# Transposes ahead of value products and scores in attention's lists, and keys' transposes ahead of intra-chunk products in the mixer

## The chip, the core and the metric

The kernel runs on one core of a Trainium2 chip. Such a core has a matrix engine (TensorE, PE in the profile; its weight loads are listed apart as PEld), a vector engine (VectorE, DVE), a scalar engine for activation functions (ScalarE, ACT), a general engine (GpSimd, POOL), and a sync engine (SP) that issues most DMAs. Each engine works through its own list of instructions in order and waits for semaphores of the others. Operands lie in SBUF; PE writes its results to PSUM, which has eight banks of 128 partitions x 512 floats, and from there ACT or DVE copy them out.

The metric is the device time of one execution, in microseconds (us); lower is better.

## The reference

Two layers of a decoder trunk on a sequence of 1024 positions and 1024 features. Layer 0 mixes tokens by dilated sliding-window attention, layer 1 by a gated linear recurrence (HGRN2) in chunks of 64; each mixer is followed by a squared-ReLU MLP, and each of the four sub-layers by a LayerNorm of the scaled input plus its output. What the change touches is inside the two mixers:

```python
def dilated_attention_mixer(x, w_in, w_out):
    proj = (x @ w_in).reshape(B, S, N_GROUPS, 3, ATTN_HEADS, ATTN_HEAD_DIM)
...
    for g, (window, dilation) in enumerate(DILATED_PATTERNS):
        q = rotary(proj[:, :, g, 0], pos)
        k = rotary(proj[:, :, g, 1], pos)
        o, lse = dilated_window_attention(q, k, proj[:, :, g, 2], window, dilation)
...
    wts = jax.nn.softmax(jnp.stack(lses, axis=0), axis=0)
    o = jnp.einsum('gbsh,gbshe->bshe', wts, jnp.stack(outs, axis=0).astype(F32))
    return o.reshape(B, S, ATTN_HEADS * ATTN_HEAD_DIM).astype(x.dtype) @ w_out

# in dilated_window_attention, on banded blocks of 128 queries
    s = jnp.einsum('znqhe,znkhe->znhqk', qb, kk).astype(F32) * (E ** -0.5)
    p = jnp.exp(s - m)
    o = jnp.einsum('znhqk,znkhe->znqhe', (p / l).astype(v.dtype), vv)

# in hgrn2_mixer, per head and chunk
    a = jnp.where(causal, jnp.einsum('bhcid,bhcjd->bhcij', q_dec, k_dec), 0.0)
    o_intra = jnp.einsum('bhcij,bhcje->bhcie', a, v)
    kv = jnp.einsum('bhcjd,bhcje->bhcde', key * jnp.exp(b_last - b), v)
```

## The kernel before

Dense products run in three passes of split floats (high x high, high x low, low x high), each a matmul of 128x128 weights with 512 columns. The rest of PE's work is small matmuls and transposes in full floats (a transpose is a matmul with the identity on the whole array).

**Attention.** The input projection is a list of products (`seq`, function `product`, L816), in each of which PE issues twelve matmuls (L826 to L828) into one of three `mm` banks. Heads are taken in pairs (8 of them), and a pair in one dilation group is a *unit*: 24 units, always in the order group 2, group 1, group 0. Two units make one round of 21 products (three outputs of seven products each). Work on units whose projection is done is put between the products: a table `fill` says for each product number which functions run behind it, a *slot*. A unit begins with step 0 four (first of a round) or fourteen (second) products into the next round and does one step every two or three products after it; the offsets are `OFFS` (L66), plus `UNIT0`. So step 5 of one unit and step 0 of the next fall into the same slot, the older unit first. The last round has no products behind it; its two units use a list of their own (the branch `tail` in `pieces`) in the output projection.

The six steps of a unit are the lists that `pieces` (L539) returns. They are made of:

- `vtrans`: eight transposes of the values, four to a `pt` bank, which ACT copies to `vn` (L551, L552).
- `qk` (L561) or, for group 2, `qk16` (L592): scores as small matmuls on a 64x64 part of the array (L573, L601) into two `s` banks; DVE adds the mask and takes the extreme (L586, L604) into a `p` tile, one of three; ACT takes the exponential with its row sum (L589, L608).
- `ptr` (L636), `ptr16` (L612): transposes of `p` into a `pt` bank (L642, L617), one of two, which ACT copies to a `pts` tile, one of four.
- `pv` (L647), `pv16` (L621): value products on 128x64 and 64x64 parts (L671, L673, L629) into the one `o` bank (`pv16` takes a `pt` bank too); ACT copies it out. `first` are blocks 0 to 3, `second` blocks 4 to 7.
- `shift`: three DMAs on the sync queue that make a copy of the values shifted by 64 rows.

PE and DVE are held to program order throughout the attention's main loop (`in_order`, L902); ACT's PSUM copies are held in the order of their making (`behind`, L986), and where else ACT stands is chosen by the framework's scheduler, which orders by program order and readiness.

**Mixer.** Per head there are six projections of 24 matmuls (L192 to L194), and between them the pieces of the head before (`head_pieces`, L1751): transposes of values and keys (`trans`, L1760, two `pt` banks each, copied by ACT), intra-chunk products (`amat`, L1768, one `s` bank, then DVE), chunk states (`kv`, L1784), outputs (`omat`, L1806, L1811) and their transposes (`otr`, L1833). Here PE's order is not written out; the scheduler chooses it. The pieces of the last head run in the output projection.

Of the kernel before, what the change touches and what calls it, by code (L numbers as in the profile page):

```python
# [69 lines left out]
def trunk_kernel(  # L70
# [32 lines left out]
    def U(name, dt=F32):  # L103
        return up.tile([P, 1024], dt, name=name, tag="u")

    def bank(tag, name):
        return ps.tile([P, 512], F32, name=name, tag=tag, bufs={"mm": 3, "s": 2, "pt": 2, "o": 1}[tag])
# [45 lines left out]
    one = cp.tile([P, 1], F32, name="one")  # L153
# [203 lines left out]
    def attention(pre, hc):  # L357
# [181 lines left out]
        def pieces(pr, g, qT, kT, vT, og, sS, tail):  # L539
# [145 lines left out]
            def qks(*tiles):  # L685
                return [lambda: qk(*tiles)]

            def run(f, bs):
                return [lambda b=b: f(b) for b in bs]

            one = [(b,) for b in range(8)]
# [8 lines left out]
                ]  # L700
            first, second = [lambda: pv(0, 1, 2, 3)], [lambda: pv(4, 5, 6, 7)]
            if g == 2:
                return [run(qk16, (0,)) + [vtrans], run(qk16, (1,)) + run(ptr16, (0,)), run(ptr16, (1,)),
                        [pv16], [], []]
            if g == 1:
                return [qks((0, 2), (4, 6)) + [vtrans], [shift] + qks((1,), (3,)) + run(ptr, ((0, 2), (4, 6))),
                        qks((5,), (7,)) + run(ptr, ((1,), (3,))), first + run(ptr, ((5,), (7,))), [], second]
            return [qks(*one[0:2]) + [vtrans], [shift] + qks(*one[2:4]) + run(ptr, one[0:2]),
                    qks(*one[4:6]) + run(ptr, one[2:4]), first + qks(*one[6:8]) + run(ptr, one[4:6]),
                    run(ptr, one[6:8]), second]  # L710

        def combine_tr(pr, g, slot, ml, tail):
# [153 lines left out]
        def unit_work(gi, a, base):  # L866
# [14 lines left out]
            def begin():  # L881
                ogs[pr][g] = U("og")
                p = pieces(pr, g, res.pop((a, 0)), res.pop((a, 1)), ep.pop((gi, 2, a)), ogs[pr][g], sS, last)
                for f in p[0]:
                    f()
                work.extend(p[1:])
# [855 lines left out]
    def hgrn(xs, late, consts, pre, gw):  # L1742
# [8 lines left out]
        def head_pieces(hd, kd, kd2, qd, vT, dec, oNt):  # L1751
            st = {}

            def trans(src, name):
                d = U(name)
                for j in range(2):
                    pt = bank("pt", "hpt")
                    for i in range(4):
                        b = j * 4 + i
                        nc.tensor.transpose(pt[:, i * P:(i + 1) * P], src[:, b * P:(b + 1) * P], ident)  # L1760
                    act(d[:, j * 512:(j + 1) * 512], pt, AF.Copy)
                st[name] = d
# [12 lines left out]
            def kv(j):  # L1775
                if j == 0:
                    st["S"] = [U("stA"), U("stB")]
                kb = [bank("s" if j else "pt", "kvps") for _ in range(2)]
                cs = [c for c in range(j * 8, j * 8 + 8) if c < NCH - 1]
                for c in cs:  # L1780
                    r = slice((c % 2) * CH, (c % 2) * CH + CH)
                    t = c // 2
                    for m in range(2):
                        nc.tensor.matmul(kb[c % 2][m * CH:m * CH + CH, (t % 4) * P:(t % 4 + 1) * P],  # L1784
                                         st["k2n"][r, t * P + m * CH:t * P + m * CH + CH],
                                         st["vn"][r, t * P:(t + 1) * P], start=True, stop=True, skip_group_check=True)
                for c in cs:
                    dst = state(c + 1)
                    kvc = kb[c % 2][:, (c // 2 % 4) * P:(c // 2 % 4 + 1) * P]
                    if c == 0:  # L1790
                        nc.vector.tensor_copy(dst, kvc)
                    else:
                        nc.vector.scalar_tensor_tensor(dst, state(c), dec[:, c:c + 1], kvc,
                                                       op0=ALU.mult, op1=ALU.add)
# [34 lines left out]
            def otr(j):  # L1829
# [8 lines left out]
            amats = [amat]  # L1838
            keys = lambda: trans(kd2, "k2n")
            return [  # L1840
                [lambda: trans(vT, "vn")] + (amats + [keys] if hd else [keys] + amats),
                [lambda: kv(0)],
                [lambda: omat(0), lambda: kv(1)],
                [lambda: omat(1)],
# [45 lines left out]
        for hd in range(8):  # L1890
# [29 lines left out]
            oNt = U("oN")  # L1920
            oN.append(ond[1, hd] if hd < SPILL[1] else oNt)
            new = head_pieces(hd, cur["kd"], cur["kd2"], cur["qd"], e[2], cur["dec"], oNt)
            if hd == 0:
                new = [[]] + new
# [110 lines left out]
```

## Time and profile before

| what | value |
|---|---|
| median of three runs | 2728.11 us (2725.67 to 2728.45) |
| the profiled execution, its own time | 2729.02 us |
| its span, first to last instruction | 2727.2 us |
| mean granted TensorE clock | 0.998 |
| attention's main loop, 80 to 905 us | PE busy 821.57 of 825.00 us, DVE 649.55, ACT 460.66 |
| mixer, 1680 to 2060 us | PE busy 379.04 of 380.00 us, DVE 225.62, ACT 199.88 |

The two rows by stage are from the view of busy time by stretches. A busy PE in that view isn't a PE at its best: matmuls overlap, so an engine that starts a matmul later than it could still counts as busy while the one before drains. What a border between two kinds of work costs has to be read from the distance between starts, in the timeline.

### The profile page before, as it was taken

What the parts mean: (1) busy time and instruction counts of PE and PEld (TensorE: products, weight loads), DVE (VectorE), ACT (ScalarE), POOL (GpSimd) and SP (SyncE); (2) the same over time, 40 slices, a digit from 0 to 9 for tenths busy, and PEclk for the clock granted to TensorE, in tenths of its full rate; (3) what the DMA queues carried; (4) which work ended last, traced back from release to release, by engine and by line L of the source; (5) the groups of instructions that cost most, each with busy time, mean ns of one, the idle gap of its engine ahead of it and who ended that gap; (6) DMA issues with size and microseconds to landing.
All of it is one profiled execution on the core that took longest, in us unless ns stands there. A gap on an engine that the chain in (4) does not pass through costs nothing.

```text
span 2727.2 us, 44137 instructions
## 1 busy us (share of the span) xinstructions
PE 2698.6 (99%) x16256; PEld 2199.0 (81%) x16256; DVE 2043.0 (75%) x3887; ACT 1387.0 (51%) x3044; POOL 28.3 (1%) x28
## 2 busy tenths in 40 slices
PE   9999999999999999999999999999999999999998
PEld 7787888888788677888888888788888888888887
DVE  8868877787787788776686686556578886678687
ACT  5555555555565456444554345556452544545443
POOL 0000000000000001000000000000000100000000
PEclk9999999999999999999999999999999999999999
DMA  7867666766867424553675652010242464485653
GB/s 297 273 225 236 210 219 204 239 224 213 257 209 237 126 105 171 186 200 137 220 253 180 221 170 93 32 62 32 74 128 110 150 224 166 152 305 176 221 177 127
DMA packets 208152, 493.66 MB, mean 181 GB/s; under 512 B 30016, under 2 KB 44864, under 8 KB 207936
## 3 DMA queue, kind: packets, MB, share of 16 engines
q1 hardware_dynamic: 206688, 489.53, 53.7%
q8 instruction: 128, 2.10, 0.3%
q10 hardware_dynamic: 1248, 1.31, 0.2%
q14 instruction: 88, 0.72, 0.1%
HBM read 362.69 MB, written 94.11 MB: 167 GB/s over the span
## 4 chain that ended last, share of the span: by engine, by line
PE 90%; DVE 6%; ACT 1%; DMA 1%; issue 1%; SPq 0%; DVEq 0%; ACTq 0%
PE pup L1351 7%; PE pup L1349 7%; PE pmm L828 7%; PE pup L1350 7%; PE pmm L826 7%; PE pmm L827 7%; PE pdy L1504 4%; PE pdy L1503 4%; PE pdy L1500 4%; PE pmm L192 3%; PE pdx L1503 3%; PE pdx L1504 3%; PE pdx L1500 3%; PE pmm L194 3%; PE pmm L193 3%; PE pmm L204 2%
## 5 line engine op out<-in xcount | busy, mean ns | idle before, releaser
L826 PE MATMUL pmm<-xh,H 128*128 128x512 f32 x1008 | 403.7, 400 | 1.6 <-ACT H L493 1.0
L828 PE MATMUL pmm<-xh,H 128*128 128x512 f32 x1008 | 395.0, 392 | 3.1 <-DVE H L501 2.9
L827 PE MATMUL pmm<-xl,H 128*128 128x512 f32 x1008 | 393.0, 390 | 0.9 <-DVE xl L158 0.9
L828 PEld LDWEIGHTS pmm<-xh,H 128*128 128x128 f32 x1008 | 189.2, 188 | 47.8 <-DVE H L501 6.9
L826 PEld LDWEIGHTS pmm<-xh,H 128*128 128x128 f32 x1008 | 189.5, 188 | 40.2 <-ACT H L493 1.9
L827 PEld LDWEIGHTS pmm<-xl,H 128*128 128x128 f32 x1008 | 189.7, 188 | 38.2 <-DVE xl L158 1.6
L1500 PE MATMUL pdy<-dT,dS 128*128 128x512 f32 x512 | 199.2, 389 | 0.0
L1503 PE MATMUL pdy<-dT,dS 128*128 128x512 f32 x512 | 199.2, 389 | 0.0
L1504 PE MATMUL pdy<-dT,dS 128*128 128x512 f32 x512 | 199.2, 389 | 0.0
L157 ACT ACTIVATE dS<-dr 128x512 fp32r<-128x512 f32 x192 | 119.4, 622 | 68.0 <-PE pdy L1504 36.2
L192 PE MATMUL pmm<-f0nh,wh 128*128 128x512 f32 x384 | 153.3, 399 | 0.0
L193 PE MATMUL pmm<-f0nl,wh 128*128 128x512 f32 x384 | 149.8, 390 | 0.0
L194 PE MATMUL pmm<-f0nh,wl 128*128 128x512 f32 x384 | 149.8, 390 | 0.0
L589 ACT ACTIVATE p<-p,stats 128x192 f32<-128x192 f32 (+1 forms) x256 | 108.9, 428 | 62.0 <-DVE stats L586 61.8
L158 DVE TENSOR_TENSOR dS<-dr,dS 128x512 fp32r<-128x512 f32 x192 | 130.9, 682 | 9.3 <-ACT dS L157 9.3
L157 ACT ACTIVATE dT<-hold 128x512 fp32r<-128x512 f32 x128 | 80.1, 625 | 80.3 <-DVE hold L1479 33.3
L1310 ACT ACTIVATE H<-wc 128x512 fp32r<-128x512 f32 x128 | 77.2, 625 | 78.4 <-DVE wc L1303 44.8
L1503 PEld LDWEIGHTS pdy<-dT,dS 128*128 128x128 f32 x512 | 96.1, 188 | 20.1
L1500 PEld LDWEIGHTS pdy<-dT,dS 128*128 128x128 f32 x512 | 96.1, 188 | 19.9
L1504 PEld LDWEIGHTS pdy<-dT,dS 128*128 128x128 f32 x512 | 96.1, 188 | 19.9
L586 DVE CUSTOM_DVE_ANT_0 p<-s,mask 128x192 f32<-128x192 f32 (+1 forms) x256 | 71.1, 337 | 45.6 <-PE s L573 32.6
L493 ACT ACTIVATE H<-wc 128x512 fp32r<-128x512 f32 x108 | 66.6, 629 | 75.3 <-DVE wc L485 73.3
(424 smaller groups left out, 6875.4 us busy)
## 6 DMA issues: line engine op xcount, KB each, us to landing
xh<-xtd SPq DMA_DIRECT2D x110, 512.0 KB
xl<-xtd SPq DMA_DIRECT2D x110, 512.0 KB
dr<-hd SPq DMA_DIRECT2D x192, 256.0 KB
dr<-in_w_down_dram SPq DMA_DIRECT2D x128, 256.0 KB
rot<-e SPq DMA_DIRECT2D x192, 128.0 KB
wa<-in_w_up_dram SPq DMA_DIRECT2D x48, 512.0 KB
wb<-in_w_attn_dram SPq DMA_DIRECT2D x36, 512.0 KB
wa<-in_w_attn_dram SPq DMA_DIRECT2D x33, 512.0 KB
```

Of the source, the lines that this page charges most:

```text
L157: act(hi, raw, AF.Copy)
L192: nc.tensor.matmul(o, wh[:, k], xs.h(k), start=k == 0, stop=False)
L193: nc.tensor.matmul(o, wh[:, k], xs.l(k), start=False, stop=False)
L194: nc.tensor.matmul(o, wl[:, k], xs.h(k), start=False, stop=k == NK - 1)
L826: nc.tensor.matmul(o, wh, hi[k // 2][:, c], start=begin and k == 0, stop=False, skip_group_check=True)
L827: nc.tensor.matmul(o, wh, lo[k // 2][:, c], start=False, stop=False, skip_group_check=True)
L828: nc.tensor.matmul(o, wl, hi[k // 2][:, c], start=False, stop=end and k == 3, skip_group_check=True)
L1349: nc.tensor.matmul(o, wh, xf.h(b, k), start=begin and k == 0, stop=False, skip_group_check=True)
L1350: nc.tensor.matmul(o, wh, xf.l(b, k), start=False, stop=False, skip_group_check=True)
L1500: nc.tensor.matmul(o[q], h, T_[:, L], start=begin, stop=False, skip_group_check=True)
L1503: nc.tensor.matmul(o[q], h, T_[:, R], start=False, stop=False, skip_group_check=True)
L1504: nc.tensor.matmul(o[q], l, T_[:, L], start=False, stop=end, skip_group_check=True)
```

## The change

In the three lists of `pieces` that the main loop uses, each step's functions are put in the order: transposes (values' or probabilities'), value products, scores. Before, scores stood ahead of the transposes, and value products ahead of both. `shift` stays first in its step, the tail's list stays. In the mixer, the keys' transposes follow the values' directly and the intra-chunk products come third; head 0 had that order before.

```diff
@@ -700,13 +700,13 @@
                 ]
             first, second = [lambda: pv(0, 1, 2, 3)], [lambda: pv(4, 5, 6, 7)]
             if g == 2:
-                return [run(qk16, (0,)) + [vtrans], run(qk16, (1,)) + run(ptr16, (0,)), run(ptr16, (1,)),
+                return [[vtrans] + run(qk16, (0,)), run(ptr16, (0,)) + run(qk16, (1,)), run(ptr16, (1,)),
                         [pv16], [], []]
             if g == 1:
-                return [qks((0, 2), (4, 6)) + [vtrans], [shift] + qks((1,), (3,)) + run(ptr, ((0, 2), (4, 6))),
-                        qks((5,), (7,)) + run(ptr, ((1,), (3,))), first + run(ptr, ((5,), (7,))), [], second]
-            return [qks(*one[0:2]) + [vtrans], [shift] + qks(*one[2:4]) + run(ptr, one[0:2]),
-                    qks(*one[4:6]) + run(ptr, one[2:4]), first + qks(*one[6:8]) + run(ptr, one[4:6]),
+                return [[vtrans] + qks((0, 2), (4, 6)), [shift] + run(ptr, ((0, 2), (4, 6))) + qks((1,), (3,)),
+                        run(ptr, ((1,), (3,))) + qks((5,), (7,)), run(ptr, ((5,), (7,))) + first, [], second]
+            return [[vtrans] + qks(*one[0:2]), [shift] + run(ptr, one[0:2]) + qks(*one[2:4]),
+                    run(ptr, one[2:4]) + qks(*one[4:6]), run(ptr, one[4:6]) + first + qks(*one[6:8]),
                     run(ptr, one[6:8]), second]
 
         def combine_tr(pr, g, slot, ml, tail):
@@ -1838,7 +1838,7 @@
             amats = [amat]
             keys = lambda: trans(kd2, "k2n")
             return [
-                [lambda: trans(vT, "vn")] + (amats + [keys] if hd else [keys] + amats),
+                [lambda: trans(vT, "vn"), keys] + amats,
                 [lambda: kv(0)],
                 [lambda: omat(0), lambda: kv(1)],
                 [lambda: omat(1)],
```

## The prediction

> **What bounds the kernel now.** I read the page first: TensorE (PE) is busy all the way, and the chain that ends last is PE.
>
> ```profile
> PE 2698.6 (99%) x16256; PEld 2199.0 (81%) x16256; DVE 2043.0 (75%) x3887; ACT 1387.0 (51%) x3044; POOL 28.3 (1%) x28
> PE 90%; DVE 6%; ACT 1%; DMA 1%; issue 1%; SPq 0%; DVEq 0%; ACTq 0%
> ```
>
> PE issues in order, so the time is the sum of the distances between its starts plus what it waits. Of the list of waits, PE alone, these are the first of 21 rows and the one that bears on the change most (total, times, longest):
>
> ```profile
> PE pmm L828 <- DVE H L501: 2.9, 5, 1.2
> ...
> PE ppt L642 <- ACT vn L361: 1.3, 3, 0.5
> ```
>
> So there is little waiting to win. What counts is how PE's starts lie at the borders between kinds of work, and that the timeline shows. I use three names: *whole* work is on the 128*128 array (products and all transposes), *small* work is on 64*64 or 128*64 parts of it (scores, value products, intra-chunk products, chunk states). A step of the attention's lists stands between two products, for example this one (start, duration, line, shape, count):
>
> ```profile
> 203.29 0.39 PE L827 MATMUL pmm<-xl,H 128*128 128x512 f32 x1
> 203.52 0.39 PE L828 MATMUL pmm<-xh,H 128*128 128x512 f32 x1
> 203.84 0.69 PE L601 MATMUL s<-kT,qT 64*64 64x64 f32 x32
> 204.46 0.66 PE L617 MATMUL ppt<-ident,p 128*128 128x128 f32 x4
> 204.87 0.48 PE L826 MATMUL pmm<-xh,H 128*128 128x512 f32 x1
> 205.19 0.39 PE L827 MATMUL pmm<-xl,H 128*128 128x512 f32 x1
> ```
>
> Two matmuls of a product are 0.23 apart. From the last product matmul's start to the second start of the next product: 0.32 into the scores, 0.62 for them with their exit, 0.41 for four transposes, 0.32 to the second product matmul, 1.67 in all. The second start belongs in the sum, since what a product's first matmul pays on entry shows only there.
>
> The trace holds the other order too, in the mixer, where a transposed output is followed by chunk states (small) and then by a product:
>
> ```profile
> 1753.55 0.39 PE L194 MATMUL pmm<-f0nh,wl 128*128 128x512 f32 x1
> 1753.79 0.60 PE L1833 MATMUL opt<-ident,on 128*128 128x128 f32 x4
> 1754.31 1.10 PE L1784 MATMUL kvps<-vn,k2n 64*64 64x128 f32 x32
> 1755.35 0.50 PE L192 MATMUL pmm<-f0nh,wh 128*128 128x512 f32 x1
> 1755.68 0.39 PE L193 MATMUL pmm<-f0nl,wh 128*128 128x512 f32 x1
> ```
>
> Product to transposes 0.24; four transposes and the way into small work 0.52; from small work into the product, first to second start, 0.33.
>
> **The change part by part.** It removes and adds no instruction. Within the attention the order of PE and of VectorE (DVE) is the order in which the program is written, so the new PE order is known. DVE's order does not change at all, since no list moves a DVE instruction past another; only its score reductions get their scores later.
>
> *(a) Simple reorderings.* A step "product, small, transposes, product" becomes "product, transposes, small, product". With the pieces above the step at 203.52 becomes 0.24 + 0.52 + 0.62 + 0.33 = 1.71 against 1.67, so **+0.04 us**. I take a small group's exit into a product to be as long as its exit into a transpose; rounding of the five rows makes it 0.02 to 0.07. The length of the small group cancels, so the figure holds for scores of every width, and for the steps with `first`, where value products and scores stay one stretch of small work. How many: the main loop has 22 units, 8 of group 2, 7 of group 1 and 7 of group 0 (the last two units use the tail's own lists, which stay). Group 2's step 1 gives 8, its step 0 only once (the others are in (b)); group 1's steps 0 to 3 give 28; group 0's steps 1 to 3 give 21. 58 x 0.04 = **2.3 us**.
>
> *(b) Joins.* By the offsets, step 5 of a unit (`second`, value products) and step 0 of the next stand in the same slot: 11 and 11 within a pair, 22 and 21+1 between pairs. Before, `second` runs into the next unit's scores without leaving small work, and the transposes come last. Now the values' transposes stand between the two: out of small work and in again.
>
> ```profile
> 196.73 0.22 PE L673 MATMUL o<-pts,vn 64*64 64x64 f32 x1
> ...
> 197.34 1.09 PE L551 MATMUL vpt<-ident,vT 128*128 128x128 f32 x8
> 198.19 0.48 PE L826 MATMUL pmm<-xh,H 128*128 128x512 f32 x1
> 198.50 0.39 PE L827 MATMUL pmm<-xl,H 128*128 128x512 f32 x1
> ```
>
> The last value product starts at 196.73 and ends at 196.95. Transposes start 0.07 ahead of the modelled end of a small group (204.46 against 203.84 + 0.69), so now at 196.88. Eight of them after small work and the way into the scores: 0.85 (197.34 to 198.19) less the 0.03 from the last one to the product (0.41 for the four at 204.46, of which four distances would be 0.44), 0.82, plus 0.20 (0.52 less three distances of 0.11), 1.02. Scores with exit 0.62 as at 203.84, second start 0.33. That ends at 198.85 where before it was 198.50: **+0.35**. Seven joins are like this (group 0 then group 2). In the other seven (group 1 then group 0) the scores have two blocks:
>
> ```profile
> 157.86 0.22 PE L673 MATMUL o<-pts,vT 64*64 64x64 f32 x1
> 157.91 0.71 PE L573 MATMUL s<-kT,qT 64*64 64x128 f32 x14
> 158.56 1.09 PE L551 MATMUL vpt<-ident,vT 128*128 128x128 f32 x8
> ...
> 159.72 0.39 PE L827 MATMUL pmm<-xl,H 128*128 128x512 f32 x1
> ```
>
> Standing alone, these scores take at least the 0.65 of their last fourteen (158.56 - 157.91) and at most the 0.81 of two wide blocks (351.68 to 352.49, below). 158.01 + 1.02 + 0.65 to 0.81 + 0.33 = 160.01 to 160.17 against 159.72: +0.29 to +0.45, I take the middle, **+0.37**. Together 7 x 0.35 + 7 x 0.37 = **5.0 us**.
>
> ```profile
> 351.68 0.88 PE L573 MATMUL s<-kT,qT 64*64 64x192 f32 x16
> 352.49 1.09 PE L642 MATMUL ppt<-ident,p 128*128 128x128 f32 x8
> ```
>
> *(c) The mixer.* Head 0 has the new order already. For heads 1 to 6 the step is now values' transposes, products in the chunk, keys' transposes, and 3.88 long (1788.21 to 1792.09):
>
> ```profile
> 1788.21 0.39 PE L194 MATMUL pmm<-f0nh,wl 128*128 128x512 f32 x1
> 1788.44 0.60 PE L1833 MATMUL opt<-ident,on 128*128 128x128 f32 x4
> 1788.87 1.04 PE L1760 MATMUL hpt<-ident,vTh 128*128 128x128 f32 x8
> 1789.84 1.15 PE L1768 MATMUL as<-qe,ls 128*64 128x64 f32 x32
> ...
> 1792.09 0.39 PE L193 MATMUL pmm<-f0nl,wh 128*128 128x512 f32 x1
> ```
>
> If the keys follow at once, it is one more of (a), +0.04. But both transposes use the two `pt` banks, and the keys' first bank is free only when ScalarE (ACT) has copied the values' first:
>
> ```profile
> 1789.70 1.08 ACT L1761 ACTIVATE vn<-hpt 128x512 f32<-128x512 f32 x2
> ```
>
> Two overlapping copies in 1.08, so the first ends near 1790.30. The keys would start at 1788.87 + 8 x 0.11 = 1789.75, so PE waits 0.55; the second bank comes free at 1790.78 and costs 0.05 more: +0.64 with the 0.04. The mixer's PE order is not written out but made by the framework's scheduler, and head 0 shows what that does with this list: it puts six chunk products between the values' and the keys' transposes.
>
> ```profile
> 1705.18 0.40 PE L194 MATMUL pmm<-f0nh,wl 128*128 128x512 f32 x1
> ...
> 1706.38 0.45 PE L1768 MATMUL as<-qe,ls 128*64 128x64 f32 x6
> ...
> 1709.13 0.39 PE L193 MATMUL pmm<-f0nl,wh 128*128 128x512 f32 x1
> ```
>
> That is 3.95, against 3.88 less the 0.43 of the transposed output that head 0 lacks: **+0.50**, the nearest row, so I take it; ends +0.04 and +0.64. Six heads: **3.0**. Head 7's list is spread over the output projection; half a head, 0 to 0.64: **0.3**.
>
> *(d) What moves besides.* The three `shift` DMAs stay first in step 1, on the same queue, and their source is copied earlier. In step 3 of groups 0 and 1 all four `pts` buffers are full when the transposes come first, so ACT's copies of them wait until `first` has read, which takes PE 1.70:
>
> ```profile
> 179.50 0.49 PE L671 MATMUL o<-pts,vn 128*64 128x128 f32 x5
> ...
> 181.20 0.37 PE L573 MATMUL s<-kT,qT 64*64 64x192 f32 x1
> ```
>
> Behind them on ACT wait exponentials, weights' high halves and the next product's copy. PE needs that bank again after the scores (0.81) and a product of twelve matmuls (12 x 0.23), more than the wait, and a product has three banks, so I cost it at nothing; uncovered it would be up to 1.70 in 14 steps, which these rows exclude. DVE's score reductions start up to 1 us later, and the weights' low halves (L501) stand behind them; they are made three products ahead, which covers it. If not, the 2.9 us of the first list grow by as much.
>
> Sum: 2.3 + 5.0 + 3.3 = **+10.6 us**. The profiled execution took 2729.02 (span 2727.2); with the sum 2739.6. It lies 0.9 above the median of the runs shown, 2728.11, so I forecast 2728.11 + 10.6 = **2738.7 us, 0.4% slower**. Stalls saved and added I take as equal (rivals two and three).
>
> **The rivals.**
>
> *One: only the number of mode changes counts.* Then (a) is free, as it has as many borders before as after, and (b) and (c), which add borders, stay: 8.3 us, 2736.4. For it speaks that leaving for small work costs alike from a product (0.32 instead of 0.23) and from a transpose (0.20 instead of 0.11). Against it speaks that coming back seems dearer into a product than into transposes, but by hardly more than the rounding of the rows, so it gets a chance of 0.15. The Trainium skill, TensorEngine Tiling (Array Packing), Key Properties, says that changing the tiling mode drains the engine; by that rule alone, with every change at one price, this rival would hold. The trace agrees with the drain: 0.09 more on each way into small work.
>
> *Two: the waits that go outweigh the borders, and it isn't slower.* Place: the transposes in step 1 of group 1 that wait for a bank. With the values' transposes at the head of step 0, their copies can be done before the exponentials and the bank is free.
>
> ```profile
> 239.05 0.88 PE L573 MATMUL s<-kT,qT 64*64 64x192 f32 x16
> 240.39 1.14 PE L642 MATMUL ppt<-ident,p 128*128 128x128 f32 x8 [0.46 <-ACT vn L361]
> ```
>
> 1.34 from scores to transposes instead of 0.81: 0.53 lost, three times by the list, 1.6 us, so 2726.5 if all borders were free. It decides where the 72 reorderings of the attention cost less than 1.6 us, 0.02 each. The rows of (b) speak against that. So do the exponentials of the same step, which end late:
>
> ```profile
> 239.67 0.19 ACT L589 ACTIVATION_READ_ACCUMULATOR p<-p,stats 128x1 f32 x1
> ```
>
> The second tile's four transposes would stand at 239.4 (238.73, the product's last start 0.32 before the scores, + 0.24 + 4 x 0.11) and wait until 239.86 anyway. Chance 0.10, mostly for a sum near zero.
>
> *Three: transposes come too early.* They stand 0.9 to 1.1 us earlier in their slot, and the scores of the step before up to 1 us later; where the exponentials end less than 2 us ahead, PE waits. In the case just shown 0.5 us lie between their end and the transposes. Where DVE and ACT aren't behind, it is 3.7 us (to 352.49, above), more than enough:
>
> ```profile
> 348.65 0.18 ACT L589 ACTIVATION_READ_ACCUMULATOR p<-p,stats 128x1 f32 x1
> ```
>
> If the three late places lost the whole 1.1 us by which transposes move, and the steps after them too, that would be 6.6: 2745.3. Chance 0.15.
>
> **How the numbers follow.** Forecast 0.60, rival one 0.15, two 0.10, three 0.15. Low end: borders at 0.02, joins at the lower figures, mixer at 0.04 and the 1.6 us won, 1.2 + 4.5 + 0.2 - 1.6 = 4.3: 2732. High end: 58 x 0.07 + 7 x 0.35 + 7 x 0.45 + 7 x 0.64 + 6.6 = 20.7: 2749. A measurement can tell about 0.2%, 5.5 us, from no change: slower from 2733.6 on. Below that lie rival two and, with 0.04, the lower end of the others: faster 0.03, same 0.11, slower 0.86.
>
> **What would show it.** In the profile after: a step like the one at 203.52 with transposes first and 1.71 long; joins with value products, transposes, scores, a product, 0.35 longer; heads 1 to 6 with chunk products split around the keys, 4.4 long; PE's waits no longer than before. A list of waits with `ppt` behind ACT `p` by many microseconds would be rival three, simple steps of equal length rival one. I would be wrong if the scheduler finds the keys' bank free, or if late copies on ACT reach PE.

## The result, and the profile after

The kernel with the change took 2746.39 us (median of 4 runs, 2743.73 to 2747.76), the kernel before beside it 2728.12 us (4 runs): ratio 1.0068, 95% interval 1.0056 to 1.008. So it is 0.7% slower; the forecast was 0.4%. The profiled executions are 14.7 us apart in their spans (2727.2 and 2741.9); why this is less than the medians' 18.3 stands in the last section. One execution of `e7_consts`, an experiment below, took 15399.9 us and is not in its ratio; why it did is open.

The page of the kernel after, busy times and the shares of the chain that ended last:

```profile
PE 2708.5 (99%) x16256; PEld 2206.2 (80%) x16256; DVE 2044.0 (75%) x3887; ACT 1390.5 (51%) x3044; POOL 30.2 (1%) x28
...
PE 87%; DVE 7%; DMA 2%; ACT 2%; issue 1%; SPq 1%; DVEq 0%; ACTq 0%
```

TensorE has the same number of instructions, its busy time grew by 10 us, and its share of the chain fell from 90% to 87%: DVE, DMA, ACT and SP's queue have each a point more. So not only borders were added, but waits too, against the forecast. The list of PE's waits says which:

```profile
PE pmm L828 <- DVE H L501: 6.1, 7, 1.4
...
PE pmm L826 <- DVE e L859: 1.7, 1, 1.7
...
PE ppt L617 <- ACT p L608: 1.3, 4, 0.3
```

The first row was 2.9, 5, 1.2 before, the third 0.8, 3, 0.3. The second is new. The row of transposes behind the values' copies (`ppt L642 <- ACT vn L361`, 1.3 us before) is gone.

First the borders. A simple reordering (start, duration, line, shape, count):

```profile
207.31 0.39 PE L828 MATMUL pmm<-xh,H 128*128 128x512 f32 x1
207.55 0.60 PE L617 MATMUL ppt<-ident,p 128*128 128x128 f32 x4
208.07 0.69 PE L601 MATMUL s<-kT,qT 64*64 64x64 f32 x32
...
209.03 0.40 PE L827 MATMUL pmm<-xl,H 128*128 128x512 f32 x1
```

Transposes first, and 1.72 from 207.31 to 209.03 where it was 1.67. A join of group 0 with group 2:

```profile
200.17 0.22 PE L673 MATMUL o<-pts,vn 64*64 64x64 f32 x1
200.32 1.09 PE L551 MATMUL vpt<-ident,vT 128*128 128x128 f32 x8
201.34 0.69 PE L601 MATMUL s<-kT,qT 64*64 64x64 f32 x32
...
202.30 0.39 PE L827 MATMUL pmm<-xl,H 128*128 128x512 f32 x1
```

From the last value product to the second start of the next product 2.13, where it was 1.77: the values' transposes cut the small work in two. And a head of the mixer, in which the chunk products are split around the keys' transposes:

```profile
1800.00 0.39 PE L194 MATMUL pmm<-f0nh,wl 128*128 128x512 f32 x1
...
1801.63 0.56 PE L1768 MATMUL as<-qe,ls 128*64 128x64 f32 x10
1802.14 1.14 PE L1760 MATMUL hpt<-ident,ze 128*128 128x128 f32 x8
1803.22 0.91 PE L1768 MATMUL as<-qe,ls 128*64 128x64 f32 x22
...
1804.39 0.39 PE L193 MATMUL pmm<-f0nl,wh 128*128 128x512 f32 x1
```

4.39 long against 3.88.

To find the rest, I took the distance between the starts of the last matmuls of two neighbouring products, for every product of the main loop, in both traces, and subtracted. TensorE does the same work in a slot in both, so what differs is a border or a wait. Two stages come out of it, each from last product matmul to last product matmul (us):

| stage | before | after | difference | forecast |
|---|---|---|---|---|
| attention's main loop | 821.67 | 836.34 | +14.67 | +7.3 |
| mixer | 341.33 | 344.18 | +2.85 | +3.3 |

| in the main loop | count | us |
|---|---|---|
| joins | 7 x 0.354, 7 x 0.347 | +4.9 |
| simple reorderings | 58, of 0.03 to 0.07, a few beside new waits up to 0.10 | +2.8 |
| steps of transposes alone, whose lists didn't change | 14 x -0.03 | -0.4 |
| new waits of products for `H` (at 410, 641, 872 us) | 1.50, 1.30, 1.68 | +4.5 |
| new wait for `e` (at 131 us) | 1 | +2.2 |
| probabilities' transposes in three late rounds (243, 474, 705 us), beyond the 0.04 of the border | 3 x 0.60 | +1.8 |
| first transposes of group 2 (at 92 us), beyond the 0.07 | 1 | +1.35 |
| small waits of before that went, and the rest | | -2.4 |

The borders make 7.3 (4.9 + 2.8 - 0.4), what was forecast. The waits make another 7.4 (4.5 + 2.2 + 1.8 + 1.35 - 2.4), and for them the forecast had nothing.

**Where the waits come from.** The largest kind, as it stands in PE's timeline (in brackets the idle time before the instruction and what ended it):

```profile
411.40 0.50 PE L828 MATMUL pmm<-xh,H 128*128 128x512 f32 x1 [1.20 <-DVE H L501]
```

DVE makes that `H` and was late because an instruction ahead of it waited:

```profile
407.39 1.23 DVE L536 TENSOR_TENSOR rot<-rot,sinT 128x1024 f32<-128x1024 f32 x1 [5.31 <-DMA rot<-e]
408.65 2.11 DVE L537 TENSOR_TENSOR qT<-qT,rot 128x1024 f32<-128x1024 f32 x1
410.62 0.73 DVE L501 TENSOR_TENSOR H<-wb,H 128x512 fp32r<-128x512 f32 x1
```

It waited 5.31 us for a DMA, the rotation's load. Before, the same instruction waited less than half of that:

```profile
398.71 1.22 DVE L536 TENSOR_TENSOR rot<-rot,sinT 128x1024 f32<-128x1024 f32 x1 [2.41 <-DMA rot<-e]
```

So look at the sync engine's queue at this place, before and after (`xh` and `xl` are the high and low parts of the input, loaded for later products):

```profile
389.32 0.50 SPq L559 DMA_DIRECT2D vT<-vn  x1
389.87 1.06 SPq L455 DMA_DIRECT2D xl<-xtd  x2
391.29 2.43 SPq L533 DMA_DIRECT2D rot<-e  x4
393.83 0.54 SPq L557 DMA_DIRECT2D vT<-vn  x1
```

```profile
387.84 0.82 SPq L455 DMA_DIRECT2D xh<-xtd  x2
394.86 0.50 SPq L557 DMA_DIRECT2D vT<-vn  x1
395.42 1.26 SPq L455 DMA_DIRECT2D xl<-xtd  x2
396.73 2.49 SPq L533 DMA_DIRECT2D rot<-e  x4
```

After, the first DMA of `shift` (L557) stands ahead of `xl` and `rot`. SP goes through its list in order, and between 388.66 (387.84 + 0.82) and 394.86 it issues nothing: it stands at L557, which needs ACT's second copy of the values. That copy ends at 394.84 (two overlapping copies in the 1.06 from 393.78), and ACT made two weight conversions and two exponentials ahead of it:

```profile
393.78 1.06 ACT L361 ACTIVATE vn<-vpt 128x512 f32<-128x512 f32 x2
```

The Trainium skill, DMA: Bandwidth & Descriptors, Anatomy of one DMA, says that a semaphore wait happens on the issuing sequencer before dispatch, and not in the DMA engines. The trace agrees: 6.2 us in which nothing of this queue was issued.

But the standstill itself isn't new. Before, the queue issued nothing from 383.34 to 389.32 either, 6.0 us, and stood at the third DMA of `shift` (L559), which also waits for a copy of the values. Counted from one and the same matmul of TensorE (389.50 before, 395.16 after), `rot` is issued 1.8 us later before and 1.6 us later after, so it is not issued later in the changed kernel. What changed is what goes out ahead of it: 256 KB at L557, where L559 has 32 KB (64 rows of 4096 and of 512 bytes), and then two `xl` of 512 KB in both. From `rot`'s first issue to DVE's start it is 10.66 us after, 7.42 before: the 3.2 us were lost between issue and landing. At the pace of before (1568 KB of these DMAs from 389.32 to 398.71) the 224 KB more would take some 1.3 us, an estimate; the rest of the 3.2 is open. The other two places look alike: 6.0 us of standstill at L559 before, 5.7 and 6.2 at L557 after.

There is little room for this: before, the `H` that TensorE used at 404.26 was ready at 402.69, 1.6 us ahead.

### The profile page after: what moved, and what is told of

It reads as the page before. It is cut to its first block, busy times and chain, and to the rows that moved or that the text cites. A ratio compares the mean times of both kernels' runs of the same rounds, so it can differ in the third digit from the quotient of the medians.

```text
span 2741.9 us, 44139 instructions
## 1 busy us (share of the span) xinstructions
PE 2708.5 (99%) x16256; PEld 2206.2 (80%) x16256; DVE 2044.0 (75%) x3887; ACT 1390.5 (51%) x3044; POOL 30.2 (1%) x28
## 4 chain that ended last, share of the span: by engine, by line
PE 87%; DVE 7%; DMA 2%; ACT 2%; issue 1%; SPq 1%; DVEq 0%; ACTq 0%
PE pup L1351 7%; PE pup L1349 7%; PE pup L1350 7%; PE pmm L826 7%; PE pmm L828 6%; PE pmm L827 6%; PE pdy L1500 4%; PE pdy L1503 4%; PE pdy L1504 4%; PE pmm L192 3%; PE pdx L1503 3%; PE pdx L1504 3%; PE pdx L1500 3%; PE pmm L193 3%; PE pmm L194 3%; PE pmm L204 2%
## 5 line engine op out<-in xcount | busy, mean ns | idle before, releaser
L828 PEld LDWEIGHTS pmm<-xh,H 128*128 128x128 f32 x1008 | 189.2, 188 | 51.1 <-DVE H L501 10.6
L1310 ACT ACTIVATE H<-wc 128x512 fp32r<-128x512 f32 x128 | 77.2, 625 | 77.4 <-DVE wc L1303 47.9
L361 ACT ACTIVATE e<-pmm 128x512 f32<-128x512 f32 x96 | 56.8, 592 | 105.5 <-PE pmm L828 105.1
```

The source lines that it names most:

```text
L828: nc.tensor.matmul(o, wl, hi[k // 2][:, c], start=False, stop=end and k == 3, skip_group_check=True)
```

## The experiments

Each is an edit of the kernel before or after, beside runs of the kernel before on the same chip.

**Which part?** Four kernels: the attention's lists alone, the mixer's list alone, and the attention's lists split into step 0 and the later steps.

`e1_attention` (the changed kernel with the mixer's old list):

```diff
-                [lambda: trans(vT, "vn"), keys] + amats,
+                [lambda: trans(vT, "vn")] + (amats + [keys] if hd else [keys] + amats),
```

> Attention's lists as in the changed kernel, the mixer as before. Borders-and-waits theory (the changed profile's 14.7 us in the attention's main loop are borders between whole and small work, about 9, and waits of PE, about 6; the mixer's 2.9 us are added by its own order alone): main loop 836.3 us as in the changed kernel, mixer (first to last head's transposes) back at 341.3, time 2.9 below the changed kernel, about 2743.5. Rival (the mixer's extra time is handed on from the attention, by buffers and DMAs that stand elsewhere): mixer stays at 344.2 and the time at 2746.4.

`e2_mixer` (the kernel before with the opposite edit):

> The mixer's order changed alone, attention as before. Borders-and-waits: each of heads 1 to 6 is 0.4 to 0.5 longer, mixer 344.2 instead of 341.3, main loop 821.7 as before, time 2728.1 + 2.9 = 2731.0. Rival (the mixer's order is free by itself): 341.3 and 2728.1.

`e3_late_steps` (the changed kernel, step 0 and the mixer as before):

```diff
-                return [[vtrans] + run(qk16, (0,)), run(ptr16, (0,)) + run(qk16, (1,)), run(ptr16, (1,)),
+                return [run(qk16, (0,)) + [vtrans], run(ptr16, (0,)) + run(qk16, (1,)), run(ptr16, (1,)),
...
-                return [[vtrans] + qks((0, 2), (4, 6)), [shift] + run(ptr, ((0, 2), (4, 6))) + qks((1,), (3,)),
+                return [qks((0, 2), (4, 6)) + [vtrans], [shift] + run(ptr, ((0, 2), (4, 6))) + qks((1,), (3,)),
...
-            return [[vtrans] + qks(*one[0:2]), [shift] + run(ptr, one[0:2]) + qks(*one[2:4]),
+            return [qks(*one[0:2]) + [vtrans], [shift] + run(ptr, one[0:2]) + qks(*one[2:4]),
```

> Steps 1 to 4 in the new order, step 0 (scores, then the values' transposes) and the mixer as before; so 50 simple reorderings and no join is broken up. Theory V (the new waits come from step 0: the values' copies on ACT and the shift's DMAs move): 50 x 0.06 = 3 us of borders and, because transposes come early in the three late rounds, 1 to 3 us of waits, main loop 826 to 828, time 2732 to 2734. Rival W (the waits come from the transposes that now stand at the head of steps 1 to 4): 3 of borders and all 6 of the waits, main loop 830.5, time 2737.

`e4_step0` (the kernel before with `[vtrans]` first in the three step 0 lists, nothing else):

> Step 0 alone in the new order (values' transposes, then scores), steps 1 to 4 and the mixer as before; 14 joins broken up and 8 simple reorderings. Theory V: 14 x 0.35 + 8 x 0.06 = 5.4 us of borders and 4 to 6 of waits (the three of some 1.4 us on the weights' low halves among them), main loop 831 to 833, time 2737.5 to 2739.5. Rival W: borders alone, main loop 827, time 2733.5.

| kernel | median, us | ratio to before (95%) | main loop | mixer |
|---|---|---|---|---|
| before (19 runs) | 2727.44 | | 821.67 | 341.33 |
| e1_attention | 2740.28 | 1.0049 (1.0034 to 1.0064) | 835.25 | 341.32 |
| e2_mixer | 2729.06 | 1.0006 (0.9997 to 1.0015) | 822.31 | 344.17 |
| e3_late_steps | 2732.51 | 1.0019 (1.0009 to 1.0028) | 823.69 | 341.35 |
| e4_step0 | 2739.53 | 1.0044 (1.0029 to 1.0059) | 831.67 | 341.32 |

The stage columns are from one profiled execution of each kernel (before: the first one), and the main loop does not repeat exactly. `e1_attention` and the changed kernel have the same order of instructions on every engine in it, and theirs are 1.1 us apart, 0.95 of it at the transposes of group 2 at 92 us (the +1.35 of the table above); before and `e2_mixer` are 0.6 apart. Single rows of that size say little.

The mixer's part is +2.84 in its stage by itself; in the whole time of `e2_mixer`, +1.6, it can't be told from no change. The later steps cost little, +2.0, at least 2 us less than I had expected: their 50 simple reorderings make 2.1 and three longer waits for the values' copies 2.9, but small waits of before went, 2.7 in all. Most of the waits come from step 0: it alone makes +10.0, of which 4.9 are its joins and 0.4 its eight simple reorderings. The two parts add up to 12.0, against 13.6 in `e1_attention`. SP's queue in `e4_step0` at the place shown above:

```profile
393.50 0.50 SPq L557 DMA_DIRECT2D vT<-vn  x1
...
395.36 2.66 SPq L533 DMA_DIRECT2D rot<-e  x4
```

and in `e3_late_steps`, where step 0 is the old one:

```profile
391.09 0.50 SPq L559 DMA_DIRECT2D vT<-vn  x1
...
392.74 2.66 SPq L533 DMA_DIRECT2D rot<-e  x4
395.51 0.54 SPq L557 DMA_DIRECT2D vT<-vn  x1
```

The order of L557 and `rot` turned round where step 0 was changed, and only there; with the old step 0 the small L559 goes first, as before. The order isn't written in the program, the scheduler chooses it. That it did so because the values are ready earlier is likely, but no run tests it.

**Taking one wait away at a time.** Three edits of the changed kernel that leave TensorE's order alone, and all three together. From here on the added lines move the line numbers by one to ten: L649 of `e6_copies`, for example, is L642 above.

`e5_rot`, the shift's DMAs behind the rotation's load on SP:

```diff
+            ahead_of["rot"] = [latest().name]      # in rope, after its four DMAs
...
-                q.dma_start(vT[0:HD, :], vn[HD:P, :])
...
+                    q.dma_start(to, src)
+                    if not tail:
+                        behind(latest(), ahead_of["rot"])
```

> The changed kernel with the three DMAs of the values' shift (vT<-vn, L557) put behind the scores' rot load on SP; TensorE's and VectorE's orders are those of the changed kernel. Theory S (the shift, moved ahead of rot on SP, makes rot late, VectorE waits 5.3 us for it and the products of L827 to L828 stand still for 1.55 to 1.75 us three times): the three stalls before L828 at 410, 641 and 872 us go or fall under 0.4 us, VectorE's wait for rot falls from 5.3 to some 2.4 us, the main loop goes from 836.3 to some 832 us, the time to some 2742 us. Rival (VectorE is late because the scores themselves come later, the DMA's order is beside the point): the three stalls stay at 1.3 to 1.8 us, the main loop stays within 1 us of 836.3.

`e6_copies`, the exponentials behind the values' copies on ACT:

```diff
+                st["copied"] = out_of[-1].name      # in vtrans
...
+            def after_copies():
+                if "copied" in st:
+                    behind(latest(), [st["copied"]])
...
+                            after_copies()      # after each exponential in qk, qk16
```

> The changed kernel with the exponentials held behind the copies of the values' transposes on ScalarE, so that the two copies no longer stand between the third and the fourth exponential; TensorE's order is that of the changed kernel. Theory C (the copies in the middle of the eight exponentials hold up the probabilities' transposes): the 8 transposes of the late rounds at 243, 474 and 705 us take 0.8 to 1.2 us instead of 1.84, the wait of 1.3 us of the transposes at 91.6 us goes, the main loop loses 3 to 4 us, to some 833 us. Rival (the transposes are simply ahead of what the exponentials can give, in whatever order): the waits move but stay, the main loop loses less than 1 us.

`e7_consts`, a chain of small DVE instructions for the next layer's constants three products earlier:

```diff
-            if n == 36:
+            if n == 33:
                 hc.append(hgrn_consts())
```

> The changed kernel with the HGRN constants' small chain issued at slot 33 instead of 36. Theory (the one stall of 2.1 us at 131 us is VectorE waiting in that chain for ScalarE's exponential, which now comes behind the group's other exponentials): the stall goes, the main loop falls from 836.3 to some 834 us. Rival (VectorE is late at 131 us for another cause): the stall stays within 0.5 us of 2.1 and so does the main loop.

`e8_all`, the three edits together:

> The changed kernel with all three edits. If the waits are what the prediction left out and the borders are what is left: the main loop falls to 826 to 829 us (821.7 of before, and 7.0 of borders less some of the waits of before), the time to some 2737 to 2739 us, still over the kernel before by 0.3 to 0.4%. Rival (the three waits hide one another or further ones behind them): the main loop stays over 831 us.

| kernel | median, us | ratio to before (95%) | main loop |
|---|---|---|---|
| before (9 runs) | 2727.64 | | 821.67 |
| e5_rot | 2742.03 | 1.0049 (1.0035 to 1.0064) | 831.87 |
| e6_copies | 2740.92 | 1.0048 (1.0033 to 1.0063) | 831.57 |
| e7_consts | 2742.10 | 1.0050 (1.0033 to 1.0067) | 834.38 |
| e8_all | 2737.31 | 1.0034 (1.0022 to 1.0047) | 828.17 |

In `e5_rot` the queue has `rot` first again, and DVE does not wait for it at this place:

```profile
392.25 2.43 SPq L533 DMA_DIRECT2D rot<-e  x4
396.21 1.91 SPq L560 DMA_DIRECT2D vT<-vn  x3
```

```profile
403.35 1.22 DVE L537 TENSOR_TENSOR rot<-rot,sinT 128x1024 f32<-128x1024 f32 x1
```

All three stalls are gone, 4.6 us with the little of one that before has too, and the loop is 4.47 shorter (836.34 - 831.87), since elsewhere some small waits went and two new ones came (+0.4 and +0.5): the order on SP was their cause. Had DVE been late because of later scores, the rival, they would have stayed. The edit takes the standstill and the 256 KB away from `rot` at once, so it doesn't divide the price between them. In the kernel before, the standstill alone cost next to nothing, as `e10_before_plus` below shows.

`e6_copies` gave 4.77, more than expected, and shows why: with the copies ahead of the exponentials, SP gets past the same DMA earlier too. `rot` is issued at 394.57, 0.7 us after the matmul counted from above and not 1.6, and DVE's wait falls to 4.21, though `rot` still takes 10.43 from issue to DVE's start:

```profile
405.00 1.22 DVE L536 TENSOR_TENSOR rot<-rot,sinT 128x1024 f32<-128x1024 f32 x1 [4.21 <-DMA rot<-e]
```

That is 1.1 less, and of PE's three stalls of 1.2, 1.2 and 1.4 us 0.1, 0.5 and nothing are left. At 92 us the wait of group 2's transposes went too, 1.3 us. The transposes of the late rounds it helped less than I had thought. After and in `e6_copies`:

```profile
242.85 2.17 PE L642 MATMUL ppt<-ident,p 128*128 128x128 f32 x8
244.95 0.72 PE L573 MATMUL s<-kT,qT 64*64 64x192 f32 x12
```

```profile
240.93 1.88 PE L649 MATMUL ppt<-ident,p 128*128 128x128 f32 x8
242.74 0.88 PE L578 MATMUL s<-kT,qT 64*64 64x192 f32 x16
```

2.10 and 1.81 from the first transpose to the scores, where eight transposes without a wait would take 0.96 (0.52 for four in the simple step, and four more at 0.11). So most of this loss is not the copies' place in the order: ACT runs the two copies and then the eight exponentials without a pause (238.29 to 242.43), and the transposes stand too early for them in either order. The rival was right there.

`e7_consts` gave 1.96, and the stall at 131 us went, 2.2 us; further waits went and came in about equal parts. In the changed kernel DVE waited 3.33 us in the middle of that chain for one small exponential, which ACT made at 126.97, behind two copies of the values and a weight's conversion; products' sums (L859) stood behind it on DVE:

```profile
127.21 0.17 DVE L1674 TENSOR_TENSOR hc_den<-hc_e 128x8 f32<-128x8 f32 x1 [3.33 <-ACT hc_e L1672]
```

Before, that wait was 0.93.

Together they give 8.2, less than the sum of 11.2 (4.47 + 4.77 + 1.96), because the first two take away the same three stalls: 3.1 us of them are in both. What is left of the main loop, +6.5, is the borders of 7.3, with waits of both signs on top; with the mixer's 2.9 it is 9.4, and the time says +9.7 (2737.31 - 2727.64). The forecast's sum was 10.6.

**Is it the border, or the early transpose?** If borders cost, then a join must become cheap when the values' transposes stand ahead of the older unit's value products, so that TensorE goes into small work only once. `e9_joins` is `e8_all` with step 0 cut in two, the first half put at the head of its slot:

```diff
-                for f in p[0]:
-                    f()
-                work.extend(p[1:])
+                p[0].pop(0)()
+                work.extend(p)
...
+                    fill.setdefault(base + UNIT0 + OFFS[a][0], []).insert(0, core.pop(0))
                     for k, f in enumerate(core):
                         at(base + UNIT0 + OFFS[a][k], f)
```

> The kernel of e8_all, but where step 0 of a unit stands in one slot with step 5 of the older one, the values' transposes come ahead of the older unit's value products: transposes, value products, scores, so that TensorE goes into small work once and not twice. If a border between whole and small work is what costs (and not that transposes stand early), each of the 14 joins falls from +0.35 us to what a simple reordering costs, 0.03 to 0.07 us: 14 times 0.3, 4.2 us less, the main loop from 828.2 to some 824 us, the time some 4 us under e8_all, to some 2733 us. Rival (the price of a join comes from the values' transposes standing ahead of the scores, whatever is in front of them): the joins stay at +0.3 to +0.35 us and the main loop at 828.

The time was 2733.15 us, against 2728.26 for before in 21 runs (ratio 1.0019, 1.001 to 1.0028), the main loop 823.45. A join now:

```profile
193.86 1.03 PE L552 MATMUL vpt<-ident,vT 128*128 128x128 f32 x8
194.82 0.27 PE L681 MATMUL o<-pts,vn 128*64 128x64 f32 x1
...
196.89 0.63 PE L610 MATMUL s<-kT,qT 64*64 64x64 f32 x30
...
197.79 0.39 PE L837 MATMUL pmm<-xl,H 128*128 128x512 f32 x1
```

Over the kernel before, the seven joins of group 0 with group 2 cost 0.054 each instead of 0.354, the other seven 0.073 instead of 0.347. The same transposes are even earlier than in the change, and all but about a fifth of the price or less is gone. What costs is one border more, not the transposes' place.

**A kernel that beats both?** `e10_before_plus` is the kernel before with the edit of `e5_rot`, and with head 0 of the mixer in the order of the others:

```diff
-                [lambda: trans(vT, "vn")] + (amats + [keys] if hd else [keys] + amats),
+                [lambda: trans(vT, "vn")] + amats + [keys],
```

> The kernel before with the shift's DMAs behind the rot load on SP, and in head 0 of the mixer the intra-chunk products ahead of the keys' transposes as in the other heads. It should take away the small waits of products for H behind DVE in the main loop of before (0.24, 0.37 and 0.66 us) as far as they come from rot, and 0.5 us in head 0: main loop 820.5 to 821.7, mixer 340.8 us, time 0.5 to 1.8 us under the kernel before, ratio 0.9993 to 0.9998. If it isn't under it, the waits for rot had been hidden in before, and head 0's order was as good.

It was the same as before: 2728.42, ratio 1.0 (0.9991 to 1.0009). The main loop is 821.28, 0.4 shorter, less than two executions of one order can differ; two of the three waits for `H` stayed, so they are not `rot`'s. `rot` is issued at 385.62 here and not at 391.29, with nothing of `shift` ahead of it, so the standstill of the kernel before had cost it next to nothing. The mixer is 341.83, 0.5 longer, although head 0's step did become 0.5 shorter. Before and in this kernel, two products of head 0's outputs:

```profile
1723.32 0.43 PE L1811 MATMUL ho<-stA,qe 128*64 128x128 f32 x2 [0.37 <-DVE stA L1793]
...
1724.71 0.43 PE L1811 MATMUL ho<-stA,qe 128*64 128x128 f32 x2 [0.59 <-DVE stA L1793]
```

```profile
1723.94 0.43 PE L1814 MATMUL ho<-stA,qe 128*64 128x128 f32 x2 [1.57 <-DVE stA L1796]
...
1725.34 0.43 PE L1814 MATMUL ho<-stA,qe 128*64 128x128 f32 x2 [0.17 <-DVE stA L1796]
```

PE comes 0.6 earlier, and DVE's chain of states 0.6 later: 0.96 of waiting became 1.74. What was won in the step was paid back there, and more. Why DVE is later I did not try. No version here beats the kernel before.

## Why the prediction was right, and where not

The sign, the mechanism and the size of the borders held. The measured +18.3 us lie inside the range (2746.39 in 2732 to 2749), above the forecast of +10.6. That the range held is in part luck: its upper end has 6.6 us for transposes that stand too early, of which some 3 came; the rest of the missing time came from DMAs and from a chain on DVE, for which it had nothing.

- *(a) Simple reorderings.* 2.3 predicted, 2.8 measured, each between 0.033 and 0.074 where 0.02 to 0.07 was given and no new wait stands beside. That group 2's steps cost 0.067 and group 1's 0.040 on average shows that the price hangs a little on the shapes beside it. Fourteen steps of transposes alone gained 0.03 each; why is open.
- *(b) Joins.* 5.0 predicted, 4.9 measured: 0.354 and 0.347 for 0.35 and 0.37. `e9_joins` shows that it is the second way into small work.
- *(c) The mixer.* 3.3 predicted, 2.85 measured. Head 1 takes 0.34 and heads 2 to 6 0.495 each for 0.50, and the chunk products are split around the keys' transposes as in head 0. Head 7, costed at 0.3, took nothing.
- *(d) What moves besides.* This is the step that failed: "The three `shift` DMAs stay first in step 1, on the same queue, and their source is copied earlier", costed at nothing. They stay in step 1, but on SP the first of them, 256 KB, came to stand ahead of `rot`, where before only the 32 KB of the third did, and `rot` reached DVE 3.2 us later after its issue: 4.5 us of stalls, taken away by `e5_rot`. The cover named for L501, three products ahead, didn't hold: the low half that was ready 1.6 us ahead of its use came some 3 us later. "If not, the 2.9 us of the first list grow by as much" is what happened: 6.1.
- *"Stalls saved and added I take as equal."* This is the term that was mis-sized: 0, measured +7.4. Beside the 4.5 there are 2.2 for a chain on DVE that waits for ACT (`e7_consts`), which the prediction did not have at all, and 3.2 for transposes ahead of their exponentials (1.35 of it at 92 us, which `e1_attention` has in small part only); 2.4 of small waits went. The bank wait that rival two counted on did go.
- *Rivals.* One (only the number of changes counts) falls: simple reorderings, which change no number, cost 2.8. Two falls: 1.6 was won, but the borders cost 7.3. Three (transposes too early) held at its three late places, nearly in size: 2.10 against 0.96, 1.1 lost at each where 1.1 was named, of which the saved bank wait pays 0.5. It is not the whole of the missing time, and the steps after those places did not lose it again.

## What to carry to other kernels

An engine that is always busy, as TensorE is here, paid for each border between kinds of work; count the ways in and out per slot, and when a piece must come earlier, move it to the head of the whole slot rather than between two pieces of the other kind. When a step moves in program order, look at every in-order queue whose order a scheduler chooses, for what may now go out ahead of what: here 256 KB used late went ahead of a load used early. And waits saved and waits added were not equal, 2.4 us against 9.8: size each before calling them so.

## What the runs showed of the hardware

The prices of borders repeat to a few nanoseconds: over the seven joins of a kind they were 353 or 354 ns after, 353 or 354 in `e4_step0`, and 53 or 54 in `e9_joins`.

Between executions TensorE's pace differs at one place by more than some of the effects. In the profiled execution of before, after waits of 1.5, 0.2 and 1.26 us, matmuls of a product start 0.43 apart and not 0.23:

```profile
1038.43 0.63 PE L1350 MATMUL pup<-af11l,H 128*128 128x512 f32 x1
1038.85 0.63 PE L1351 MATMUL pup<-af11h,H 128*128 128x512 f32 x1
```

In that of after, a longer wait at the same place (1.90 us) is followed by the full pace:

```profile
1051.98 0.39 PE L1350 MATMUL pup<-af11l,H 128*128 128x512 f32 x1
1052.21 0.40 PE L1351 MATMUL pup<-af11h,H 128*128 128x512 f32 x1
```

In the view of busy time by stretches, the granted clock (after PE, PEld, DVE, ACT and POOL) of these places is 0.59 before and 1.00 after:

```profile
1032.00:1040.00 8.00, 6.54 (x22) 4.25 (x22) 7.83 (x14) 3.04 (x7) 1.27 (x1) 0.59 0.68 257
```

```profile
1048.00:1056.00 8.00, 5.75 (x24) 4.11 (x23) 7.03 (x12) 2.77 (x6) 0.50 (x1) 1.00 0.50 182
```

From the main loop's end to the mixer's first head, the stretch that holds this place, before's profiled execution took 2.7 us longer than that of after, and those of the experiments 0.4 (`e7_consts`, at the full pace too) to 2.6. This is most of why the profiled executions are 14.7 us apart and the medians 18.3. The Trainium skill, TensorE: Matmul & The Clock Gate, Part 1, tells of a gate with two states, half and full clock, set by how busy the array was in a free-running window; the two paces and their chance appearance agree with it. What set the gate at this place no run shows.
